# Weight parts placed at different offsets in their buffers, and three orders of wide and narrow products in the up projection

## The chip, the core and the metric

The kernel runs on one core of a Trainium2 chip. The metric is device time in microseconds, the median of several executions. A profile of one execution comes from the hardware profiler; its span runs from the first instruction to the last, and the granted clock of TensorE is shown beside it.

## What is computed

One decoder layer with conditioning, on 256 tokens of width 2048, float32 in and out. A vector c gives shifts, scales and gates; the hidden state goes through an input projection, a retention branch and an HGRN2 branch with gates, an output projection, and then a feed-forward part with a causal convolution of three taps.

```python
mod = silu(c) @ w_ada + b_ada            # shift1, scale1, gate1, shift2, scale2, gate2
h   = rms_norm(x, g_norm1) * (1 + scale1) + shift1
p   = h @ w_in                           # q,k,v,g of retention | q,f,i,g of HGRN2 | gates A, B
yA  = (head_layer_norm(retention(rope(q), rope(k), v)) * silu(g)) @ w_ret_o
yB  = (head_rms_norm(hgrn2(silu(q), f, i)) * silu(g)) @ w_hg_o
x   = x + gate1 * ((sigmoid(gA) * yA + sigmoid(gB) * yB) @ w_out)
h2  = rms_norm(x, g_norm2) * (1 + scale2) + shift2
a, b = split(causal_depthwise_conv3(h2 @ w_up))
x   = x + gate2 * ((silu(a) * b) @ w_down)
out = rms_norm(x, g_final)
```

## The kernel before

**Two parts for each operand.** All large products are made in TensorE's float32r format, from operands split into an upper and a lower part. A weight piece (two tiles of 128 contraction rows by 512 columns) is loaded by SyncE into one of 12 buffers `raw` (`load`, L156 to L159). ScalarE writes the upper part `wh` (L169), VectorE the lower part `wl = raw - wh` (L174). There are 4 buffers each of `wh` and `wl`, 4096 bytes a partition, taken in turn. Activations (`hT`, `og`, `mT`, `h2T`, `gs`) are blocks of 4096 bytes in a pool of 27 (tag `k4`), each holding two contraction tiles, and for each the 256 upper values and then the 256 lower ones. Three products are summed for each tile: upper by upper, lower activation by upper weight, upper activation by lower weight.

**Three forms.** `mm_rows` (L192 to L203) holds the activation as the stationary operand and streams 512 columns of weights: L198 upper activation by wh, L199 lower activation by wh, L203 upper activation by wl. It makes the row groups of the input projection, the branch gates (wab), the branch output projections (whg, wret), the output projection (wout) and the down projection (wdown). `mm_cols` (L205 to L218) holds weights and streams 256 columns of activation, three times. `mm_wide` (L220 to L228) and `up_group` hold weights and stream the 512 columns of an activation tile, both parts at once, against wh (a wide product: L225, L1125), and then 256 columns, the upper part, against wl (a narrow one: L228, L1127).

**The up projection.** `up_group` runs 22 times, once for every two tiles of each half of the 2 x 5632 columns: 16 contraction tiles, 4 output tiles of 128 columns, in PSUM tiles `pg` and `po` by turns. For each contraction tile it makes two wide products, the two narrow ones for the same outputs, and so for the other two outputs. `wide_group` makes the retention's q and k (4 groups) in runs of eight wide and eight narrow products.

**Order.** The matmuls, loads and splits stand in program order per engine, or in an order that the tile scheduler chose from a program traced piece by piece; background work (the conditioning products, which use `raw` buffers too, L458, and the two branches) is pumped in between at a set pace. `pieces` yields a piece's parts after asking for its split.

Of the kernel before, what the change touches and what calls it, by code (L numbers as in the profile page):

```python
# [36 lines left out]
NOSYNC = mybir.DependencyInfo(mybir.DependencyClass.NoSync, mybir.DependencyReason.DATA)  # L37
SMALL = 70

C_RQ, C_RK, C_RV, C_RG, C_HQ, C_HF, C_HI, C_HG = (i * W1 for i in range(8))  # L40
# [17 lines left out]
class Kernel:  # L58
# [96 lines left out]
    def load(self, src, m, w):  # L155
        self.n += 1  # L156
        raw = self.wp.tile([P, m, w], F32, name=f"raw_{self.n}", tag="raw", bufs=12)
        self.pin(self.nc.sync.dma_start(out=raw, in_=src))
# [18 lines left out]

    def pieces(self, src, kts, gain=None):

        uppers = []  # L180
        for k in range(0, kts, 2):
            m = min(2, kts - k)

            while len(uppers) <= k // 2 + (gain is not None) and 2 * len(uppers) < kts:
                at = 2 * len(uppers)
                z = min(2, kts - at)
                uppers.append(self.upper(src[:, at : at + z, :], z, G, gain))
# [41 lines left out]

    def wide_group(self, src, act):  # L230
# [5 lines left out]
        pieces = self.pieces(src, KT)  # L236
# [12 lines left out]

    def products(self, mm, ps, src, act, k0, kts, hold=0, first=True, last=True, gain=None):  # L250

        held = []
        for step in self.pieces(src[:, k0 : k0 + kts, :], kts, gain):
# [11 lines left out]
    def rows(self, src, act, k0=0, kts=KT, ps=None):  # L265
        return self.parts(self.products(self.mm_rows, ps or self.pg(), src, act, k0, kts), True)

# [526 lines left out]
    def run(self):  # L794
# [74 lines left out]
        self.pace(0, 3.5, 24)  # L869

        work = 2 * FIRST
        g = FIRST
# [6 lines left out]
        while min(done) < KT:  # L879
# [7 lines left out]
            if m > 0:  # L887
                self.finish(*ada[:have])
                if g < RESIDENT:
                    self.products(mms[g], ps[g], a["wa"][g], act, done[g], m, first=False, last=have == KT)  # L890
                    if have == KT:
                        take(g, ps[g], True)
                else:
                    take(g, self.products(mms[g], self.pg(), a["wa"][g], act, done[g], m), done[g] == 0)
                done[g] = have
# [45 lines left out]
        for j in range(4):  # L941
            for at, z in self.rows(a["whg"][j], lambda k: og[0][k // 2][:, k % 2, :], 0, 8):
                nc.vector.tensor_tensor(sgb[j][:, at, :], sgb[j][:, at, :], z, ALU.mult)
# [13 lines left out]
        for j in range(4):  # L957
            for at, z in self.rows(a["wret"][j], lambda k: og[1][k // 2][:, k % 2, :], 0, 8):
                nc.vector.tensor_tensor(sga[j][:, at, :], sga[j][:, at, :], z, ALU.mult)
# [15 lines left out]
        for j in range(4):  # L975
# [6 lines left out]
            elif last:  # L982
                g = g3
            ps = self.products(self.mm_rows, self.po2() if last else self.pg(), a["wout"][j], actm, 0, KT, hold=4 * last, gain=g if last else None)
            if last:
                g = None
                self.finish(ada2)
                up = self.pieces(a["wup"][0], KT)
                up = chain([next(up), next(up)], up)
# [68 lines left out]
        for i in range(FT // 2):  # L1058
# [51 lines left out]
    def up_group(self, i, act2, gT, pieces, begun=None):  # L1110
# [6 lines left out]
        else:  # L1117
            ps = [self.po() for _ in range(4)]
        for step in pieces:
            for kt, wh, wl in step:  # L1120
                act = act2(kt)
                for j in range(0, 4, 2):
                    cs = [slice(z * P, (z + 1) * P) for z in (j, j + 1)]
                    for z in range(2):
                        self.pin(nc.tensor.matmul(ps[j + z], lhsT=wh[:, cs[z]], rhs=act, start=kt == 0, stop=False, skip_group_check=bool(begun)))  # L1125
                    for z in range(2):
                        nc.tensor.matmul(ps[j + z][:, :T], lhsT=wl[:, cs[z]], rhs=act[:, :T], start=False, stop=kt == KT - 1, skip_group_check=bool(begun))  # L1127
            self.pump(len(step) / 2)
# [19 lines left out]
    def down(self, gT, x1, g2):  # L1148
# [15 lines left out]
        for j in range(4):  # L1164
# [127 lines left out]
```

## Time and profile before

| what | value |
|---|---|
| median of 3 runs | 1511.69 us (1511.67 to 1511.91) |
| the profiled execution | 1511.24 us |
| its span | 1509.5 us |
| TensorE matmuls | 8466, busy 1493.7 us |
| VectorE | busy 1211.9 us |
| ScalarE | busy 841.7 us |
| mean DMA rate | 256 GB/s |

A row of the page's groups gives the line, the engine, the operation, what is written and read, the count, the busy time, the mean length of one, and the idle time of the engine ahead of it with what ended it. PE is TensorE's matmul, PEld its weight load, which overlaps the matmul. Matmuls overlap each other too, since their recorded length holds their way through the array: the distance from one start to the next is what a stream of them costs, and the sum of lengths is not. The timeline view lists starts and merges equal instructions that follow each other.

### The profile page before, as it was taken

Reading aid. Unit: us, or ns where it says so; the run is one execution under the profiler, and the core shown is the slowest. Engines: PE = TensorE matmul, PEld = TensorE weight load, DVE = VectorE, ACT = ScalarE, POOL = GpSimd, SP = SyncE. Lnnn points to the kernel's source line nnn. Section 1 sums busy time; section 2 is a strip of 40 time slices with the busy share of each in tenths; the row PEclk is TensorE's granted clock in tenths of the full one; section 3 lists DMA queues with packets and bytes.
Section 4 is the critical chain, followed back from the end, with each engine's and each line's share of the span. In section 5 each row is a group of like instructions: output and inputs, shape, how many; then the busy total and the mean of one; then the engine's idle time right before and its main releaser. Section 6 shows DMA issues by size and latency. Waiting matters only on the chain.

```text
span 1509.5 us, 22703 instructions
## 1 busy us (share of the span) xinstructions
PE 1493.7 (99%) x8466; PEld 1275.5 (84%) x8466; DVE 1211.9 (80%) x1647; ACT 841.7 (56%) x1210; POOL 4.0 (0%) x8
## 2 busy tenths in 40 slices
PE   8999999999999999999999999999999999999997
PEld 6889899888888888888888888888888888888886
DVE  7899997998999877898977778777777769455784
ACT  6745456767775644455466555555555658344342
POOL 0000000000000000000000000000000000000000
PEclk9999999999999999999999999999999999999999
DMA  9999997777887899989847777777777666667651
GB/s 373 376 347 336 321 320 257 265 248 274 281 278 262 285 302 326 318 290 361 298 132 242 229 233 230 230 231 238 229 239 231 216 193 204 197 206 212 183 171 56
DMA packets 110994, 385.71 MB, mean 256 GB/s; under 512 B 12802, under 2 KB 13346, under 8 KB 110884
## 3 DMA queue, kind: packets, MB, share of 16 engines
q1 hardware_dynamic: 110016, 383.14, 76.7%
q8 instruction: 66, 1.08, 0.3%
q10 hardware_dynamic: 868, 1.13, 0.2%
q14 instruction: 44, 0.36, 0.1%
HBM read 382.11 MB, written 2.11 MB: 255 GB/s over the span
## 4 chain that ended last, share of the span: by engine, by line
PE 93%; DVE 3%; ACT 1%; issue 1%; DMA 1%; SPq 0%; DVEq 0%; ACTq 0%
PE pg L198 13%; PE pg L203 13%; PE pg L199 13%; PE po L1125 11%; PE pg L1125 10%; PE po L1127 5%; PE pg L1127 5%; PE pg L225 4%; PE po L198 3%; PE po L203 3%; PE po L199 3%; PE pg L228 2%; DVE wl L174 1%; DVE raw L458 1%; PE po L218 1%
## 5 line engine op out<-in xcount | busy, mean ns | idle before, releaser
L174 DVE TENSOR_TENSOR wl<-raw,wh 128x1024 fp32r<-128x1024 f32 (+1 forms) x536 | 633.1, 1191 | 233.6 <-ACT wh L169 230.6
L169 ACT ACTIVATE wh<-raw 128x1024 fp32r<-128x1024 f32 (+1 forms) x536 | 547.9, 1033 | 482.5 <-PE pg L199 167.0
L458 DVE SCALAR_TENSOR_TENSOR raw<-raw,sc 128x1024 f32<-128x1024 f32 x192 | 233.8, 1222 | 0.1
L1125 PE MATMUL po<-h2T,wh 128*128 128x512 f32 x704 | 221.1, 395 | 0.0
L1125 PE MATMUL pg<-h2T,wh 128*128 128x512 f32 x688 | 216.4, 396 | 0.0
L198 PE MATMUL pg<-wh,hT 128*128 128x512 f32 x512 | 202.1, 395 | 0.9 <-DVE p L830 0.6
L199 PE MATMUL pg<-wh,hT 128*128 128x512 f32 x512 | 199.8, 390 | 0.0
L1127 PEld LDWEIGHTS po<-h2T,wl 128*128 128x128 f32 x704 | 132.3, 188 | 31.3
L1127 PEld LDWEIGHTS pg<-h2T,wl 128*128 128x128 f32 x688 | 129.2, 188 | 31.0 <-DVE wl L174 0.5
L203 PE MATMUL pg<-wl,hT 128*128 128x512 f32 x512 | 138.4, 390 | 0.1
L1127 PE MATMUL po<-h2T,wl 128*128 128x256 f32 x704 | 138.3, 278 | 0.0
L1127 PE MATMUL pg<-h2T,wl 128*128 128x256 f32 x688 | 135.3, 278 | 0.1
L198 PEld LDWEIGHTS pg<-wh,hT 128*128 128x128 f32 x512 | 96.1, 188 | 21.3 <-ACT f L579 1.0
L203 PEld LDWEIGHTS pg<-wl,hT 128*128 128x128 f32 x512 | 96.0, 188 | 20.6 <-DVE wl L174 0.4
L199 PEld LDWEIGHTS pg<-wh,hT 128*128 128x128 f32 x512 | 96.2, 188 | 19.6 <-DVE hT L387 0.3
L1125 PEld LDWEIGHTS po<-h2T,wh 128*128 128x128 f32 x704 | 107.2, 189 | 0.0
L1125 PEld LDWEIGHTS pg<-h2T,wh 128*128 128x128 f32 x688 | 104.7, 189 | 0.0
L199 PE MATMUL pg<-wh,gs 128*128 128x512 f32 x176 | 68.6, 390 | 0.0
L198 PE MATMUL pg<-wh,gs 128*128 128x512 f32 x176 | 68.5, 389 | 0.0
L198 PE MATMUL po<-wh,gs 128*128 128x512 f32 x176 | 68.5, 389 | 0.0
L199 PE MATMUL po<-wh,gs 128*128 128x512 f32 x176 | 68.5, 389 | 0.0
L225 PE MATMUL pg<-hT,wh 128*128 128x512 f32 x256 | 65.1, 396 | 0.2 <-DVE p L247 0.2
(255 smaller groups left out, 2023.3 us busy)
## 6 DMA issues: line engine op xcount, KB each, us to landing
raw<-in_wup SPq DMA_DIRECT2D x176, 512.0 KB, 4.5
raw<-in_wdown SPq DMA_DIRECT2D x88, 512.0 KB, 4.2
raw<-in_wa SPq DMA_DIRECT2D x80, 512.0 KB, 5.7
raw<-in_ada SPq DMA_DIRECT2D x64, 512.5 KB, 5.4
raw<-in_ada SPq DMA_DIRECT2D x64, 512.0 KB, 5.5
raw<-in_wab SPq DMA_DIRECT2D x64, 512.0 KB, 5.0
raw<-in_gate SPq DMA_DIRECT2D x32, 512.5 KB, 4.3
raw<-in_wk SPq DMA_DIRECT2D x32, 512.0 KB, 5.1
```

Source lines behind the costliest of these rows:

```text
L169: self.pin(self.nc.scalar.activation(wh, raw, AF.Copy))
L174: self.last = self.nc.vector.tensor_tensor(wl, raw, wh.bitcast(F32), ALU.subtract)
L198: nc.tensor.matmul(ps[t], lhsT=act[:, hi], rhs=wh, start=first and i == 0, stop=False)
L199: nc.tensor.matmul(ps[t], lhsT=act[:, lo], rhs=wh, start=False, stop=False)
L203: nc.tensor.matmul(ps[t], lhsT=act[:, hi], rhs=wl, start=False, stop=last and i == len(items) - 1)
L218: nc.tensor.matmul(outs[j], lhsT=wl[:, cs[j]], rhs=act[:, :T], start=False, stop=last and i == len(items) - 1, skip_group_check=True)
L225: nc.tensor.matmul(ps[z], lhsT=wh[:, z * P : (z + 1) * P], rhs=act, start=first and i == 0, stop=False)
L228: nc.tensor.matmul(ps[z][:, :T], lhsT=wl[:, z * P : (z + 1) * P], rhs=act[:, :T], start=False, stop=last and i == len(items) - 1)
L458: dot = self.pin(nc.vector.scalar_tensor_tensor(raw[:, 0, :], raw[:, 0, :], 1.0, self.sc[:, u * GW : u * GW + w], ALU.mult, ALU.mult, accu ...
L1125: self.pin(nc.tensor.matmul(ps[j + z], lhsT=wh[:, cs[z]], rhs=act, start=kt == 0, stop=False, skip_group_check=bool(begun)))
L1127: nc.tensor.matmul(ps[j + z][:, :T], lhsT=wl[:, cs[z]], rhs=act[:, :T], start=False, stop=kt == KT - 1, skip_group_check=bool(begun))
```

## The change

`wh` and `wl` buffers grow from 4096 to 4352 bytes a partition (64 floats more), and each part starts at a byte offset in its buffer that is set by tables, one pair (for wh, for wl) for each weight group: `COLS` for the four column groups of the input projection, `WIDES` for the four retention groups, `ROWSAT` (the same offset for both parts) for the 20 groups of wab, whg, wret and wout, `UPS` for the 22 groups of the up projection, and `DOWNS` for the four of the down projection. The eight row groups of the input projection stay at offset 0. To make room, `raw` has 11 buffers in place of 12. In `up_group` the first number of a group's entry in `UPS` sets how many wide products run ahead of their narrow ones: 2 as before (groups 0 to 6), 8 (7 to 13), 16 (14 to 18; two pieces are then taken together), or 1 (19 to 21).

```diff
@@ -36,6 +36,16 @@
+ROWSAT = (4, 12, 20, 24, 40, 56, 72, 100, 116, 132, 140, 148, 152, 156, 176, 240, 108, 112, 116, 0)
+UPS = (
+    (2, 192, 192), (2, 64, 192), (2, 192, 64), (2, 144, 64), (2, 0, 64), (2, 48, 64), (2, 64, 160),
+    (8, 0, 64), (8, 0, 0), (8, 0, 192), (8, 144, 64), (8, 192, 64), (8, 192, 192), (8, 64, 64),
+    (16, 0, 64), (16, 144, 64), (16, 192, 64), (16, 0, 160), (16, 0, 192),
+    (1, 0, 0), (1, 64, 64), (1, 192, 192),
+)
+WIDES = ((0, 64), (192, 64), (0, 192), (144, 64))
+COLS = ((64, 64), (160, 160), (192, 192), (8, 8))
+DOWNS = ((0, 64), (64, 0), (0, 112), (0, 0))
...
-        raw = self.wp.tile([P, m, w], F32, name=f"raw_{self.n}", tag="raw", bufs=12)
+        raw = self.wp.tile([P, m, w], F32, name=f"raw_{self.n}", tag="raw", bufs=11)
         self.pin(self.nc.sync.dma_start(out=raw, in_=src))
         return raw
 
-    def upper(self, src, m, w, gain=None):
+    def part(self, name, m, w, shift):
+
+        full = self.wp.tile([P, 2 * G + 64], F32R, name=f"{name}_{self.n}", tag=name, bufs=4)
+        return full[:, shift // 4 : shift // 4 + m * w].rearrange("p (m w) -> p m w", m=m)
+
+    def upper(self, src, m, w, gain=None, shift=(0, 0)):
 
         raw = self.load(src, m, w)
         if gain is not None:
             self.pin(self.nc.vector.tensor_tensor(raw, raw, gain[:, None, :].to_broadcast([P, m, w]), ALU.mult))
         self.n += 1
-        wh = self.wp.tile([P, m, w], F32R, name=f"wh_{self.n}", tag="wh", bufs=4)
-        wl = self.wp.tile([P, m, w], F32R, name=f"wl_{self.n}", tag="wl", bufs=4)
+        wh, wl = [self.part(n, m, w, at) for n, at in zip(("wh", "wl"), shift)]
...
-            begin(self.retention, hb, *[self.wide_group(a["wk"][2 * hb + i], act) for i in range(2)], v.pop(0))
+            begin(self.retention, hb, *[self.wide_group(a["wk"][2 * hb + i], act, WIDES[2 * hb + i]) for i in range(2)], v.pop(0))
...
-            for at, z in self.rows(a["wab"][j], act):
+            for at, z in self.rows(a["wab"][j], act, shift=(ROWSAT[j],) * 2):
...
-            self.up_group(i, act2, gT, up if i == 0 else self.pieces(a["wup"][i], KT), pu if i == 0 else None)
+            self.up_group(i, act2, gT, up if i == 0 else self.pieces(a["wup"][i], KT, shift=UPS[i][1:]), pu if i == 0 else None)
...
+        run = UPS[i][0]
         for step in pieces:
-            for kt, wh, wl in step:
-                act = act2(kt)
-                for j in range(0, 4, 2):
-                    cs = [slice(z * P, (z + 1) * P) for z in (j, j + 1)]
-                    for z in range(2):
-                        self.pin(nc.tensor.matmul(ps[j + z], lhsT=wh[:, cs[z]], rhs=act, start=kt == 0, stop=False, skip_group_check=bool(begun)))
-                    for z in range(2):
-                        nc.tensor.matmul(ps[j + z][:, :T], lhsT=wl[:, cs[z]], rhs=act[:, :T], start=False, stop=kt == KT - 1, skip_group_check=bool(begun))
+            step = list(step)
+            if run == 16 and not begun:
+                step += next(pieces)
+            some = [(kt, act2(kt), wh, wl, z) for kt, wh, wl in step for z in range(4)]
+            for at in range(0, len(some), run):
+                part = some[at : at + run]
+                for kt, act, wh, wl, z in part:
+                    self.pin(nc.tensor.matmul(ps[z], lhsT=wh[:, z * P : (z + 1) * P], rhs=act, start=kt == 0, stop=False, skip_group_check=bool(begun)))
+                for kt, act, wh, wl, z in part:
+                    nc.tensor.matmul(ps[z][:, :T], lhsT=wl[:, z * P : (z + 1) * P], rhs=act[:, :T], start=False, stop=kt == KT - 1, skip_group_check=bool(begun))
...
-            ps = self.products(self.mm_rows, (self.pg, self.po2)[j % 2](), a["wdown"][j], act, 0, FT, hold=8 * last, gain=g if last else None)
+            ps = self.products(self.mm_rows, (self.pg, self.po2)[j % 2](), a["wdown"][j], act, 0, FT, hold=8 * last, gain=g if last else None, shift=DOWNS[j])
```

The calls for `COLS`, for whg, wret and wout, and the parameter that hands an offset pair down (`shift`) through `pieces`, `products`, `rows` and `wide_group`, are changed in the same way.

The order of matmuls on TensorE is the same up to the up projection. At the start of its group 8 (entry 8 in `UPS`; `pg` are the PSUM outputs, `h2T` the activation tile, `wh` and `wl` the weight parts; "x2" stands for two equal rows) TensorE had, before the change:

```order
L1125 MATMUL pg_9236<-h2T_7344,wh_9240 128x512 x2
L1127 MATMUL pg_9236<-h2T_7344,wl_9241 128x256 x2
L1125 MATMUL pg_9237<-h2T_7344,wh_9240 128x512 x2
L1127 MATMUL pg_9237<-h2T_7344,wl_9241 128x256 x2
L1125 MATMUL pg_9236<-h2T_7344,wh_9240 128x512 x2
L1127 MATMUL pg_9236<-h2T_7344,wl_9241 128x256 x2
L1125 MATMUL pg_9237<-h2T_7344,wh_9240 128x512 x2
L1127 MATMUL pg_9237<-h2T_7344,wl_9241 128x256 x2
```

and has now, with line numbers moved by the added lines:

```order
L1147 MATMUL pg_9236<-h2T_7344,wh_9240 128x512 x2
L1147 MATMUL pg_9237<-h2T_7344,wh_9240 128x512 x2
L1147 MATMUL pg_9236<-h2T_7344,wh_9240 128x512 x2
L1147 MATMUL pg_9237<-h2T_7344,wh_9240 128x512 x2
L1149 MATMUL pg_9236<-h2T_7344,wl_9241 128x256 x2
L1149 MATMUL pg_9237<-h2T_7344,wl_9241 128x256 x2
L1149 MATMUL pg_9236<-h2T_7344,wl_9241 128x256 x2
L1149 MATMUL pg_9237<-h2T_7344,wl_9241 128x256 x2
```

The narrow products, which stood behind each two wide ones, now stand behind eight, those of both contraction tiles of a piece.

At the start of group 14, TensorE had two pieces one after the other, of which these are the first and the beginning of the next contraction tiles:

```order
L1125 MATMUL pg_10550<-h2T_7344,wh_10554 128x512 x2
L1127 MATMUL pg_10550<-h2T_7344,wl_10555 128x256 x2
L1125 MATMUL pg_10551<-h2T_7344,wh_10554 128x512 x2
L1127 MATMUL pg_10551<-h2T_7344,wl_10555 128x256 x2
L1125 MATMUL pg_10550<-h2T_7344,wh_10554 128x512 x2
L1127 MATMUL pg_10550<-h2T_7344,wl_10555 128x256 x2
L1125 MATMUL pg_10551<-h2T_7344,wh_10554 128x512 x2
L1127 MATMUL pg_10551<-h2T_7344,wl_10555 128x256 x2
L1125 MATMUL pg_10550<-h2T_7345,wh_10576 128x512 x2
L1127 MATMUL pg_10550<-h2T_7345,wl_10577 128x256 x2
```

and has now the wide products of two pieces (two `wh` buffers) ahead of the first narrow one:

```order
L1147 MATMUL pg_10550<-h2T_7344,wh_10554 128x512 x2
L1147 MATMUL pg_10551<-h2T_7344,wh_10554 128x512 x2
L1147 MATMUL pg_10550<-h2T_7344,wh_10554 128x512 x2
L1147 MATMUL pg_10551<-h2T_7344,wh_10554 128x512 x2
L1147 MATMUL pg_10550<-h2T_7345,wh_10560 128x512 x2
L1147 MATMUL pg_10551<-h2T_7345,wh_10560 128x512 x2
L1147 MATMUL pg_10550<-h2T_7345,wh_10560 128x512 x2
L1147 MATMUL pg_10551<-h2T_7345,wh_10560 128x512 x2
L1149 MATMUL pg_10550<-h2T_7344,wl_10555 128x256 x2
L1149 MATMUL pg_10551<-h2T_7344,wl_10555 128x256 x2
L1149 MATMUL pg_10550<-h2T_7344,wl_10555 128x256 x2
L1149 MATMUL pg_10551<-h2T_7344,wl_10555 128x256 x2
```

The first narrow product moved from the third place to the seventeenth.

In group 19, where the outputs are four tiles `po`, TensorE had:

```order
L1125 MATMUL po_11641<-h2T_7344,wh_11647 128x512
L1125 MATMUL po_11642<-h2T_7344,wh_11647 128x512
L1127 MATMUL po_11641<-h2T_7344,wl_11648 128x256
L1127 MATMUL po_11642<-h2T_7344,wl_11648 128x256
L1125 MATMUL po_11643<-h2T_7344,wh_11647 128x512
L1125 MATMUL po_11644<-h2T_7344,wh_11647 128x512
L1127 MATMUL po_11643<-h2T_7344,wl_11648 128x256
L1127 MATMUL po_11644<-h2T_7344,wl_11648 128x256
```

and has now:

```order
L1147 MATMUL po_11641<-h2T_7344,wh_11647 128x512
L1149 MATMUL po_11641<-h2T_7344,wl_11648 128x256
L1147 MATMUL po_11642<-h2T_7344,wh_11647 128x512
L1149 MATMUL po_11642<-h2T_7344,wl_11648 128x256
L1147 MATMUL po_11643<-h2T_7344,wh_11647 128x512
L1149 MATMUL po_11643<-h2T_7344,wl_11648 128x256
L1147 MATMUL po_11644<-h2T_7344,wh_11647 128x512
L1149 MATMUL po_11644<-h2T_7344,wl_11648 128x256
```

Each narrow product now follows the wide one of the same output, so that consecutive matmuls write the same PSUM tile. On VectorE some splits (`wl`) exchange places with neighbouring steps of the convolution in the up projection; no instruction is added or removed on any engine.

More of the change, by code (lines that the diff above doesn't have):

```diff
@@ L176, in rest, with pieces @@
         return wh, wl
-    def pieces(self, src, kts, gain=None):
+    def pieces(self, src, kts, gain=None, shift=(0, 0)):
         uppers = []
@@ L186, in pieces @@
                 z = min(2, kts - at)
-                uppers.append(self.upper(src[:, at : at + z, :], z, G, gain))
+                uppers.append(self.upper(src[:, at : at + z, :], z, G, gain, shift))
             wh, wl = self.rest(uppers[k // 2])
@@ L228, in mm_wide, with wide_group @@
                 nc.tensor.matmul(ps[z][:, :T], lhsT=wl[:, z * P : (z + 1) * P], rhs=act[:, :T], start=False, stop=last and i == len(items) - 1)
-    def wide_group(self, src, act):
+    def wide_group(self, src, act, shift=(0, 0)):
         nc = self.nc
@@ L235, in wide_group @@
         steps = list(range(0, KT, 4))
-        pieces = self.pieces(src, KT)
+        pieces = self.pieces(src, KT, shift=shift)
         for k in steps:
@@ L248, in wide_group, with products @@
         return out
-    def products(self, mm, ps, src, act, k0, kts, hold=0, first=True, last=True, gain=None):
+    def products(self, mm, ps, src, act, k0, kts, hold=0, first=True, last=True, gain=None, shift=(0, 0)):
         held = []
-        for step in self.pieces(src[:, k0 : k0 + kts, :], kts, gain):
+        for step in self.pieces(src[:, k0 : k0 + kts, :], kts, gain, shift):
             items = [(act(k0 + kt), wh, wl) for kt, wh, wl in step]
@@ L263, in products, with rows @@
         return ps
-    def rows(self, src, act, k0=0, kts=KT, ps=None):
-        return self.parts(self.products(self.mm_rows, ps or self.pg(), src, act, k0, kts), True)
+    def rows(self, src, act, k0=0, kts=KT, ps=None, shift=(0, 0)):
+        return self.parts(self.products(self.mm_rows, ps or self.pg(), src, act, k0, kts, shift=shift), True)
     def put_split(self, dst, src):
@@ L869, in run, with visit @@
         self.pace(0, 3.5, 24)
+        cols = [g for g in range(len(ATT)) if ATT[g] not in ROWS]
+        def visit(g):
+            return COLS[cols.index(g)] if g in cols else (0, 0)
         work = 2 * FIRST
@@ L889, in run @@
                 if g < RESIDENT:
-                    self.products(mms[g], ps[g], a["wa"][g], act, done[g], m, first=False, last=have == KT)
+                    self.products(mms[g], ps[g], a["wa"][g], act, done[g], m, first=False, last=have == KT, shift=visit(g))
                     if have == KT:
@@ L893, in run @@
                 else:
-                    take(g, self.products(mms[g], self.pg(), a["wa"][g], act, done[g], m), done[g] == 0)
+                    take(g, self.products(mms[g], self.pg(), a["wa"][g], act, done[g], m, shift=visit(g)), done[g] == 0)
                 done[g] = have
@@ L941, in run @@
         for j in range(4):
-            for at, z in self.rows(a["whg"][j], lambda k: og[0][k // 2][:, k % 2, :], 0, 8):
+            for at, z in self.rows(a["whg"][j], lambda k: og[0][k // 2][:, k % 2, :], 0, 8, shift=(ROWSAT[8 + j],) * 2):
                 nc.vector.tensor_tensor(sgb[j][:, at, :], sgb[j][:, at, :], z, ALU.mult)
@@ L957, in run @@
         for j in range(4):
-            for at, z in self.rows(a["wret"][j], lambda k: og[1][k // 2][:, k % 2, :], 0, 8):
+            for at, z in self.rows(a["wret"][j], lambda k: og[1][k // 2][:, k % 2, :], 0, 8, shift=(ROWSAT[12 + j],) * 2):
                 nc.vector.tensor_tensor(sga[j][:, at, :], sga[j][:, at, :], z, ALU.mult)
@@ L983, in run @@
                 g = g3
-            ps = self.products(self.mm_rows, self.po2() if last else self.pg(), a["wout"][j], actm, 0, KT, hold=4 * last, gain=g if last else None)
+            ps = self.products(self.mm_rows, self.po2() if last else self.pg(), a["wout"][j], actm, 0, KT, hold=4 * last, gain=g if last else None, shift=(ROWSAT[16 + j],) * 2)
             if last:
@@ L987, in run @@
                 self.finish(ada2)
-                up = self.pieces(a["wup"][0], KT)
+                up = self.pieces(a["wup"][0], KT, shift=UPS[0][1:])
                 up = chain([next(up), next(up)], up)
```

## The prediction, made before the changed kernel ran

> **What bounds the kernel now.** I read the page first: engine totals, slices, chain.
>
> ```profile
> span 1509.5 us, 22703 instructions
> PE 1493.7 (99%) x8466; PEld 1275.5 (84%) x8466; DVE 1211.9 (80%) x1647; ACT 841.7 (56%) x1210; POOL 4.0 (0%) x8
> PEclk9999999999999999999999999999999999999999
> PE 93%; DVE 3%; ACT 1%; issue 1%; DMA 1%; SPq 0%; DVEq 0%; ACTq 0%
> ```
>
> TensorE is busy 99% of the span at a full granted clock, and 93% of the chain that ended last is matmuls. Only some 16 us of the span (1509.5 - 1493.7) have no matmul in them. So the time is a count of matmuls times the distance from one start to the next, and nothing but that distance can be worth much. I read it from the timeline of TensorE, whose first column is the start and whose second is the length in us, in the rows form of the products (a down group, 512 moving columns each) and in the columns form (256 columns).
>
> ```profile
> 1299.43 1.07 PE L203 MATMUL pg<-wl,gs 128*128 128x512 f32 x4
> ...
> 1302.15 1.07 PE L203 MATMUL pg<-wl,gs 128*128 128x512 f32 x4
> ...
> 1304.87 1.07 PE L203 MATMUL pg<-wl,gs 128*128 128x512 f32 x4
> ```
> ```profile
> 30.41 0.64 PE L218 MATMUL pg<-hT,wl 128*128 128x256 f32 x4
> 30.89 0.28 PE L214 MATMUL pg<-hT,wh 128*128 128x256 f32 x1
> ```
>
> From one group of four L203 to the next are 4 + 8 = 12 matmuls in 2.72 us: 226.7 ns each. Four matmuls of 256 columns start 0.48 us apart: 120.0 ns each. The 256 further columns cost 106.7 ns, 0.417 ns per column; what is left is a **constant of 13.3 ns** per matmul (226.7 - 512 x 0.417; 120.0 - 256 x 0.417). That constant is all that a change of addresses can reach. What runs in it is seen by setting the weight loads of TensorE beside the matmuls.
>
> ```profile
> 1300.34 0.39 PE L198 MATMUL pg<-wh,gs 128*128 128x512 f32 x1
> 1300.34 0.19 PEld L199 LDWEIGHTS pg<-wh,gs 128*128 128x128 f32 x1
> ```
>
> The load for the next matmul starts in the same hundredth of a microsecond as the matmul before it, so two reads of the state buffer, moving and stationary, begin together. In the kernel before, both begin at the same residue: wh, wl and every activation tile are blocks of 4096 bytes laid end to end, and slices inside them are multiples of 512 bytes. Whether the constant depends on that distance no row of this trace shows, since in the weight products it is a multiple of 512 bytes. What it shows is that the stall is not the same for like matmuls (lengths in ns, least/median/most):
>
> ```profile
> L1125 PE MATMUL po<-h2T,wh x704: 393/396/398, 794.0 to 1261.7; 128*128 128x512 f32 x176
> L1127 PE MATMUL po<-h2T,wl x704: 274/277/283, 794.4 to 1262.0; 128*128 128x256 f32 x176
> L203 PE MATMUL po<-wl,gs x176: 388/389/389, 1323.9 to 1501.4; 128*128 128x512 f32 x176
> L228 PE MATMUL pg<-hT,wl x256: 277/283/289, 291.3 to 388.6; 128*128 128x256 f32 x128
> ```
>
> 512 columns take from 388 to 398 ns, 256 columns from 274 to 283 in one stage: a **spread of 9 to 10 ns** that hangs on what is loaded beside them and when. In the rows form all are alike (389), although their distances run through several multiples of 512.
>
> **The change, part by part.**
>
> *Offsets.* They change no count and no shape. I counted pairs (matmul, and the load of the next one that runs beside it) in the changed kernel's order: of 7424 pairs of weight products, 4999 get a distance that is no multiple of 256 bytes; 2425 keep one that is. What a pair gains or loses has no row. Bounds from the nearest: the spread of 9 ns, either way, for every shifted pair: -9 x 4999 = -45.0 us to +45.0 us. The nearest row is the steady 389 ns, unmoved by distances of 512, 1024 and 2048 bytes, so I stay near zero, and below it, since both reads now begin at the same residue, the start at which two streams collide if place matters at all, while the narrow products show that 9 ns less can be had. I take a fifth of the spread: -1.8 x 4999 = **-9.0 us**.
>
> The Trainium skill (TensorE: Matmul & The Clock Gate, section Back-to-back issue gap) gives a warm matmul its columns divided by 2.4 GHz plus about 2.5 ns. The trace agrees on the columns (0.417 ns) and has 13.3 in place of 2.5; if the shifted pairs all fell to the page's figure, an estimate by it is 10.8 x 4999 = 54 us less.
>
> *Order in the up projection.* Seven groups keep pairs (2 wide, 2 narrow), seven go to eight and eight, five to sixteen, three to one and one. Pairs and eights both stand in the trace: the up projection, and the retention projections (L225, L228).
>
> ```profile
> 1000.17 0.63 PE L1125 MATMUL pg<-h2T,wh 128*128 128x512 f32 x2
> ...
> 1011.32 0.62 PE L1125 MATMUL pg<-h2T,wh 128*128 128x512 f32 x2
> ```
> ```profile
> 302.49 1.11 PE L228 MATMUL pg<-hT,wl 128*128 128x256 f32 x8
> ...
> 308.08 1.11 PE L228 MATMUL pg<-hT,wl 128*128 128x256 f32 x8
> ```
>
> Pairs: 11.15 us over 16 cycles, 696.9 ns for two wide and two narrow. Eights: 5.59 us for two cycles, 698.8 ns for the same work. A group has 32 such cycles, so eights cost 7 x 32 x 1.9 ns = **+0.4 us**. Sixteens tend to the steady 2 x 226.7 + 2 x 120.0 = 693.3 ns: between -0.6 and +0.3 us for five groups, taken as 0. One and one has no row; a pair of wide and narrow may land anywhere in the spread, 3 x 64 x 9 ns = 1.7 us either way, taken as 0 because pairs and eights differ so little.
>
> *One buffer of raw weights fewer, larger parts.* SyncE waits for a free raw tile almost all the time, and that is its slack:
>
> ```profile
> SPq L158 <- DVE wl L174: 866.5, 491, 7.1
> raw<-in_wa SPq DMA_DIRECT2D x80, 512.0 KB, 5.7
> 30.00:120.00 90.00, 89.71 (x466) 76.75 (x466) 79.90 (x105) 53.77 (x79) 0.95 (x1) 1.00 0.98 364
> 290.00:390.00 100.00, 99.75 (x917) 87.41 (x916) 94.14 (x132) 66.79 (x106) 1.91 (x2) 1.00 0.82 277
> 790.00:1230.00 440.00, 440.00 (x2528) 383.89 (x2527) 335.35 (x504) 248.76 (x376) 0.00 (x0) 1.00 0.73 230
> ```
>
> (Windows: length, busy us of PE, weight loads, DVE, ACT, POOL, clock, DMA share, GB/s.) Where transfers are densest, 30 to 120 us, 364 GB/s move one 524,288-byte tile in 1.44 us; eleven tiles are 15.8 us ahead of a landing that takes 5.7. The later loads have longer. Where loads and splits exchange places with neighbours, the same cover holds. Price 0; the cover is those 10 us, and if it is gone each late tile costs TensorE up to 1.4 us.
>
> *ACT and DVE on shifted parts.* They write and read wh and wl at the new starts. No row has such a start. The split on DVE takes 1224 ns in the median and at most 1271:
>
> ```profile
> L174 DVE TENSOR_TENSOR wl<-raw,wh x536: 670/1224/1271, 17.4 to 1491.1; 128x1024 fp32r<-128x1024 f32 x167, 128x512 fp32r<-128x512 f32 x12
> ```
>
> At +47 ns a piece, 176 pieces of the up projection add 8.3 us to a DVE that is busy 335 of 440 us there: hidden by matmuls. The thin cover is 290 to 390 us (DVE 94.1 of 100): 32 pieces, at most 1.5 us. A gain there has the same bound, and TensorE, not DVE, sets the end. Price 0.
>
> Sum: 1511.24 (the profiled execution, 1509.5 span and 1.7 around it) - 9.0 + 0.4 = 1502.6 us. The median of the runs shown is 1511.69, 0.03% above that execution; I leave it there.
>
> **The rivals.**
>
> *No effect (same).* The constant is the price of any load beside a matmul, whatever its place. For it: the rows form stands at 389 ns through all distances it has. Against: the spread in the up projection, though that may come from timing alone. Price: order alone, -1.9 to +2.4 us about 1511.6. The Trainium skill speaks for it (SBUF — State Buffer, section SBUF: two separate sides): TensorE has ports of its own and never waits on anyone, and its two read ports are independent. By that rule the offsets give 1511.6; the trace's 13.3 ns does not decide it.
>
> *Slower: shifted reads settle at the long end.* Like matmuls already show 398 ns in place of 389 in the up projection. If a distance that is no multiple of 256 makes that the steady state in a fifth of the shifted pairs more than are relieved, the price is 9 x 1000 = +9.0 us: 1520.6. It decides from the point where more pairs lengthen than shorten; then rows-form groups show matmuls over 389 ns. For it: of the wide products in the up projection all but few are on the long side, so 389 may be the lucky state; against it: nothing shows that place makes it.
>
> *The change hardly does what it says.* 2425 pairs, among them all eight row groups of the first projection, keep multiples of 256; if those alone decided, the result is that of no effect.
>
> **How the numbers follow.** Faster as forecast 0.42 (1502.6; its own range from 1476, -9 ns x four fifths of the shifted pairs, up to 1508), no effect 0.31 (1511.6), slower 0.27 (1520.6, its tail to the +45 bound). About 0.2% (3 us) is what a measurement of this kernel can tell from no change; so faster 0.42, same 0.31, slower 0.27. The range that leaves out two in ten, mostly the far ends of -45 and +45: 1482 to 1523 us.
>
> **What would show it.** In the changed profile the groups have one offset each, so the timeline tells each apart. Right: row groups with offsets start every 217 to 226 ns in place of 226.7, and differ from each other, while the unshifted down group (the last) stays at 226.7. No effect: 226.7 everywhere. Slower: lengths over 389 in the rows form. Order: a group of eights with both offsets 0 takes 32 x 0.699 = 22.4 us, one of ones with both 0 within 0.6 us of that. Buffers: PE idle on a transfer between 30 and 120 us would show that term wrong. The forecast fails if the offset's effect has one sign for nearly all distances, since then a fifth of the spread is far too little, or the wrong side.

## The result, and the profile after

The changed kernel takes 1523.35 us in the median of 3 runs (1522.72 to 1523.99), against 1511.69 us: a ratio of 1.0077, 95% interval 1.0054 to 1.0100. It is slower by 0.8%; the forecast was 1502.6 us and faster.

First the page of the changed kernel: span, engine totals, granted clock by slices, and the chain that ended last.

```profile
span 1521.5 us, 22677 instructions
...
PE 1504.9 (99%) x8466; PEld 1277.9 (84%) x8466; DVE 1209.5 (79%) x1647; ACT 841.3 (55%) x1210; POOL 4.0 (0%) x8
...
PEclk9999999999999999999999999999999999999999
...
PE 93%; DVE 2%; DMA 2%; ACT 2%; issue 1%; SPq 0%; DVEq 0%; ACTq 0%
```

The picture is that of before: TensorE busy for 99% of the span, the same 8466 matmuls, the same clock, 93% of the chain. Its busy time is 11.2 us longer (1504.9 - 1493.7) in a span that is 12.0 us longer. So no engine has become a new bound; the same matmuls follow each other at a greater distance. The view of what TensorE waited for agrees (longest waits of the changed kernel; total, times, longest):

```profile
PE po L228 <- ACT hT L396: 2.4, 2, 1.2
PE po L310 <- DMA crow<-in_c: 2.3, 1, 2.3
PE po L363 <- DVE rq L359: 1.9, 1, 1.9
```

All its waits sum to 8.6 us in eight entries, and to 7.7 us in eight before, seven of them the same. The loss must be in the stream. The view by line gives the lengths of like matmuls (least/median/most, ns) and the first and last start. One row of the kernel before, and three of the changed one (L203 is now L217):

```profile
L203 PE MATMUL pg<-wl,og x128: 387/389/398, 588.9 to 676.8; 128*128 128x512 f32 x128
```
```profile
L217 PE MATMUL pg<-wl,gs x176: 387/394/397, 1273.8 to 1453.6; 128*128 128x512 f32 x176
...
L217 PE MATMUL po<-wl,gs x176: 388/389/397, 1334.9 to 1513.5; 128*128 128x512 f32 x176
...
L217 PE MATMUL pg<-wl,og x128: 390/396/404, 593.2 to 683.7; 128*128 128x512 f32 x128
```

The two branch projections (`og`) ran from 588.9 to 676.8, 87.9 us; they now take 90.5 us (593.2 to 683.7), and not one of their 128 products with wl is as short as the old median of 389 ns: the least is 390. In the down projection the median of `pg`, groups 0 and 2, whose wl start at 64 and 112, is 394, while `po`, groups 1 and 3, whose wl both start at 0, keeps 389. The timeline shows it in single groups (start, length). First wab's last group, offset 100, then the down projection's last, offset 0:

```profile
575.98 1.12 PE L217 MATMUL pg<-wl,hT 128*128 128x512 f32 x4
...
578.86 1.12 PE L217 MATMUL pg<-wl,hT 128*128 128x512 f32 x4
```
```profile
1480.15 1.07 PE L217 MATMUL po<-wl,gs 128*128 128x512 f32 x4
...
1482.87 1.07 PE L217 MATMUL po<-wl,gs 128*128 128x512 f32 x4
```

Twelve matmuls in 2.88 us against twelve in 2.72: **240.0 ns each at offset 100, 226.7 at offset 0**. The constant of 13.3 ns has doubled to 26.6.

Summed over the whole trace, by weight groups (distance from each matmul's start to the next one's, added up in ns and given in us; the group of a matmul follows from its place in the program's order):

| products | before | after | difference |
|---|---|---|---|
| rows: wab | 178.06 | 183.55 | +5.49 |
| rows: whg and wret | 87.82 | 90.49 | +2.66 |
| rows: wout | 87.40 | 89.26 | +1.87 |
| rows: down | 239.24 | 241.56 | +2.32 |
| columns of the input projection | 96.49 | 95.09 | -1.40 |
| retention's q and k | 91.36 | 91.19 | -0.17 |
| up projection | 491.66 | 492.62 | +0.96 |

The rows form alone has +12.3 us, as much as the whole span has grown. What holds weights as the stationary operand is nearly even.

Two rows of the up projection in the changed kernel, wide and narrow:

```profile
L1147 PE MATMUL po<-h2T,wh x704: 387/392/403, 802.6 to 1271.5; 128*128 128x512 f32 x176
```
```profile
L1149 PE MATMUL po<-h2T,wl x704: 276/281/286, 803.0 to 1271.8; 128*128 128x256 f32 x176
```

The wide ones are 4 ns shorter in the median (396 before), the narrow ones 4 ns longer (277 before): gains and losses that cancel over 22 groups. The split on VectorE, which writes and reads the shifted parts, did not change (1224 and 1271 ns before):

```profile
L188 DVE TENSOR_TENSOR wl<-raw,wh x536: 666/1221/1278, 17.6 to 1503.2; 128x1024 fp32r<-128x1024 f32 x167, 128x512 fp32r<-128x512 f32 x12
```

### The profile page after: what moved, and what is told of

Read it like the earlier page. It is cut to its first block, busy times and chain, and to the rows that moved or that the text cites. A ratio compares the mean times of both kernels' runs of the same rounds, so it can differ in the third digit from the quotient of the medians.

```text
span 1521.5 us, 22677 instructions
## 1 busy us (share of the span) xinstructions
PE 1504.9 (99%) x8466; PEld 1277.9 (84%) x8466; DVE 1209.5 (79%) x1647; ACT 841.3 (55%) x1210; POOL 4.0 (0%) x8
## 4 chain that ended last, share of the span: by engine, by line
PE 93%; DVE 2%; DMA 2%; ACT 2%; issue 1%; SPq 0%; DVEq 0%; ACTq 0%
PE pg L212 13%; PE pg L217 13%; PE pg L213 13%; PE po L1147 11%; PE pg L1147 10%; PE po L1149 5%; PE pg L1149 5%; PE pg L239 4%; PE po L212 3%; PE po L213 3%; PE po L217 3%; PE pg L242 2%; PE pg L229 1%; PE pg L228 1%; PE pg L232 1%; DVE wl L188 1%
## 5 line engine op out<-in xcount | busy, mean ns | idle before, releaser
L213 PE MATMUL pg<-wh,hT 128*128 128x512 f32 x512 | 201.7, 394 | 0.0
L1147 PE MATMUL po<-h2T,wh 128*128 128x512 f32 x704 | 199.7, 393 | 0.0
L1147 PE MATMUL pg<-h2T,wh 128*128 128x512 f32 x688 | 193.0, 395 | 0.0
L217 PE MATMUL pg<-wl,hT 128*128 128x512 f32 x512 | 140.6, 394 | 0.1
L1147 PEld LDWEIGHTS po<-h2T,wh 128*128 128x128 f32 x704 | 122.8, 188 | 18.7
L1147 PEld LDWEIGHTS pg<-h2T,wh 128*128 128x128 f32 x688 | 118.5, 188 | 16.3
L1149 PE MATMUL po<-h2T,wl 128*128 128x256 f32 x704 | 125.9, 280 | 0.0
L1149 PEld LDWEIGHTS po<-h2T,wl 128*128 128x128 f32 x704 | 110.9, 188 | 11.3
L1149 PEld LDWEIGHTS pg<-h2T,wl 128*128 128x128 f32 x688 | 107.2, 188 | 14.4 <-DVE wl L188 0.6
L1149 PE MATMUL pg<-h2T,wl 128*128 128x256 f32 x688 | 116.9, 281 | 0.1
L217 PEld LDWEIGHTS pg<-wl,hT 128*128 128x128 f32 x512 | 96.6, 189 | 21.8 <-DVE wl L188 0.4
L213 PEld LDWEIGHTS pg<-wh,hT 128*128 128x128 f32 x512 | 96.7, 189 | 20.9 <-DVE hT L401 0.3
L213 PE MATMUL pg<-wh,gs 128*128 128x512 f32 x176 | 68.8, 391 | 0.0
L213 PE MATMUL po<-wh,gs 128*128 128x512 f32 x176 | 68.8, 391 | 0.0
```

The costliest lines, as they stand in the source:

```text
L213: nc.tensor.matmul(ps[t], lhsT=act[:, lo], rhs=wh, start=False, stop=False)
L217: nc.tensor.matmul(ps[t], lhsT=act[:, hi], rhs=wl, start=False, stop=last and i == len(items) - 1)
L1147: self.pin(nc.tensor.matmul(ps[z], lhsT=wh[:, z * P : (z + 1) * P], rhs=act, start=kt == 0, stop=False, skip_group_check=bool(begun)))
L1149: nc.tensor.matmul(ps[z][:, :T], lhsT=wl[:, z * P : (z + 1) * P], rhs=act[:, :T], start=False, stop=kt == KT - 1, skip_group_check=bool(be ...
```

## The experiments

The questions were, one after the other: do the offsets of the rows form make the whole loss (theory A), or do the larger buffers or the up projection make some of it? And, in the rows form, is it the **distance** between the start of the moving operand and the start of the next stationary one that decides (theory D), or **where the moving operand starts** (theory M)? In the changed kernel both change together, since weights at offset s move past activations at offset 0: the distance is then no multiple of 256, and the start itself is shifted. "Distance" is always meant modulo 256 bytes below. The means are those of a group's distances from start to start, with pauses over 300 ns left out.

### 1. Only the rows form back at offset 0

```diff
-ROWSAT = (4, 12, 20, 24, 40, 56, 72, 100, 116, 132, 140, 148, 152, 156, 176, 240, 108, 112, 116, 0)
+ROWSAT = (0,) * 20
-DOWNS = ((0, 64), (64, 0), (0, 112), (0, 0))
+DOWNS = ((0, 0),) * 4
```

> The changed kernel with every offset of the rows form at 0 (branch gates, branch outputs, output and down projection); offsets of the columns form, the retention groups and the up projection, its orders and the eleven raw buffers stay. Theory A (the loss lies in the rows form, where the shifted weights are the moving operand): the starts of these groups in the two profiles differ by 12.4 us in sum, so 1523.35 - 12.4 = 1510.9 us, and all rows groups start every 226.7 ns again. Theory B (the loss comes from the larger buffers, one raw buffer fewer or the orders in the up projection, and the rows only show it): at most half comes back, 1517 us or more.

Measured: 1510.63 us, against 1511.36 for the kernel before on the same chip; ratio 0.9995 (0.9985 to 1.0004). The whole loss is gone, with every other offset and order still there. The row by line of this kernel:

```profile
L217 PE MATMUL pg<-wl,gs x176: 389/389/389, 1263.0 to 1440.4; 128*128 128x512 f32 x176
```

All alike at 389 ns, as before the change. The columns have -1.7 us and the up projection +1.0 us here, so they nearly cancel.

### 2. Only the buffers

```diff
-COLS = ((64, 64), (160, 160), (192, 192), (8, 8))
+COLS = ((0, 0),) * 4
```

and so for the other four tables, with all 22 groups of the up projection in pairs: what is left of the change is larger parts and 11 raw buffers.

> All offsets 0 and pairs in every up group; what is left of the change is the 4352-byte parts and the eleven raw buffers. Theory A: 1511.7 us, within 1 us of the kernel before, since distances are multiples of 256 bytes and loads have slack. Theory B (buffers cost something): 1514 us or more, with TensorE idle on a transfer or on a split between 30 and 300 us.

Measured: 1511.37 against 1511.36 us, ratio 1.0003 (0.9993 to 1.0013). The window where transfers are densest, in this kernel (length, busy us of PE, weight loads, DVE, ACT, POOL, clock, DMA share, GB/s):

```profile
30.00:120.00 90.00, 89.71 (x466) 76.69 (x465) 79.80 (x106) 53.64 (x78) 0.95 (x1) 1.00 0.99 358
```

TensorE is busy for 89.71 of 90 us, the same as before: the missing raw buffer is not felt.

### 3. A scan of offsets

```diff
+ROWSAT = (16, 32, 48, 64, 80, 96, 128, 144, 160, 192, 208, 224, 8, 28, 44, 60, 240, 176, 36, 84)
+COLS = ((4, 4), (12, 12), (24, 24), (40, 40))
+DOWNS = ((4, 4), (8, 8), (64, 64), (128, 128))
```

The tables of the retention and up groups were changed too, to offsets of 0, 4, 8, 12, 24, 40, 72 and 136 bytes.

> Other offsets in every group, to complete the table: rows form at multiples of 16, and at 8, 28, 36, 44, 60, 84 bytes; columns form at 4, 12, 24 and 40; retention and up groups at 0, 4, 8, 12, 24, 40, 72 and 136 in pairs, eights and sixteens. If the place within 16 bytes decides (theories D and M alike), rows at 36, 84 and 4 stand at 240 ns, at 28, 44, 60 at 229 to 231, at 8 at 233 to 235, and all multiples of 16 at one value between 226.7 and 231. If the place within 256 bytes decides, multiples of 16 differ among themselves by more than 5 ns and 4, 36 and 84 do not agree. Columns form: 24 and 40 (8 modulo 16) stand at 115 to 116 ns as 8 did, 4 and 12 on either side of 120. Total about 1520 us.

One run, 1529.03 us, 9 us more than was expected. No rows group with an offset came near 226.7 ns: multiples of 16 gave 229 to 235 (64: 229.4, 16: 231.6, 128: 232.4, 208: 234.5), starts 12 past a multiple of 16 gave 229 to 230, those 8 past gave 233, those 4 past 235 to 238. So a start on a multiple of 16 isn't enough: its distance still costs. Nor does the offset alone set the price: 64 cost 229.4 ns in wab and 233.3 in the down projection. A full group of the up projection took 22.12 to 22.56 us (22.29 at 0). For the columns a guess of mine was missed: 24 and 40 gave 121.9 and 119.1 ns (120 at 0), so the gain seen at offset 8 in the changed kernel (115.6) is not one of all starts 8 past a multiple of 16.

### 4. The two theories apart, a first try

```diff
-                z = self.blk([P, 2, 2 * T], F32R, name="gs")
+                z = self.blk([P, 4 * T + 16], F32R, name="gs")[:, GSAT // 4 : GSAT // 4 + 4 * T].rearrange("p (j t) -> p j t", j=2)
```

with `GSAT = 12`, and `DOWNS = ((12, 12), (0, 0), (16, 16), (8, 8))`: the activation of the down projection is moved too, so that distance and start can be chosen apart.

> As the kernel with all offsets 0, but the activation tiles of the down projection (gs, the stationary operand there) start 12 bytes into their blocks, and the weight parts of its four groups at 12, 0, 16 and 8 bytes. Matmul starts in steady runs, group by group. Theory D (the distance from the moving to the stationary operand decides, modulo 16): distances 0, 12, 12 and 4, so 226.7, 240, 240 and 229 to 231 ns. Theory M (the start of the moving operand alone decides, modulo 16): 229 to 231, 226.7, 226.7 to 231 and 233 to 235 ns. Theory S (the start of the stationary operand alone): all four alike and away from 226.7 ns.

One run, 1524.65 us: 231.3, 232.4, 233.3 and 234.0 ns for the four groups. This is neither theory's pattern. The fault was in the kernel: the activation blocks had become 4160 bytes, 65 times 64, so distances ran through all multiples of 64 from tile to tile, whatever the offsets. The run decides nothing between D and M. It shows one thing all the same: in wab, whg, wret and wout, whose weights start at 0, the groups rose to means of 230 to 232 ns (226.7 to 228.6 before), so a start on a multiple of 16, even of 64, isn't enough by itself. The next two have blocks of 4352 bytes, a multiple of 256, and 9 raw buffers to make room.

### 5. Activation at 4

The edit of experiment 4 with `4 * T + 64`, `GSAT = 4`, and `DOWNS = ((4, 4), (0, 0), (8, 8), (20, 20))`.

> All offsets 0 but in the down projection. Activation blocks are 4352 bytes here (and raw has nine buffers), so that distances between blocks stay multiples of 256 bytes. The stationary gs starts 4 bytes into its block in all four groups; the weights (moving) start at 4, 0, 8 and 20 bytes. Distances moving to stationary: 0, 4, -4, -16. Theory D (what matters is that the distance is a multiple of 256): the first group 226.7 ns, all others above 229. Theory M (the moving operand's own start within 16 bytes): 240, 226.7, 233 and 240 ns.

One run, 1520.17 us. The timeline of its down groups 0, 2 and 3 (L213 is the product with wl):

```profile
1289.28 1.11 PE L213 MATMUL pg<-wl,gs 128*128 128x512 f32 x4
...
1292.13 1.11 PE L213 MATMUL pg<-wl,gs 128*128 128x512 f32 x4
```
```profile
1409.96 1.09 PE L213 MATMUL pg<-wl,gs 128*128 128x512 f32 x4
...
1412.75 1.09 PE L213 MATMUL pg<-wl,gs 128*128 128x512 f32 x4
```
```profile
1472.13 1.12 PE L213 MATMUL po<-wl,gs 128*128 128x512 f32 x4
...
1475.01 1.12 PE L213 MATMUL po<-wl,gs 128*128 128x512 f32 x4
```

Twelve matmuls take 2.85, 2.79 and 2.88 us: 237.5, 232.5 and 240.0 ns; the means of whole groups are 237.2, 232.8 and 239.9, and 232.4 for group 1. Group 0 has distance 0 and is slow: D alone falls. Group 1 has weights at 0, as in the kernel before, but the distance is 4: it is slow too, and M alone falls. Both matter. The unshifted wout groups, whose activations also lie in blocks of 4352 bytes, stay at 226.7 (three of the four; the first has 227.9, and 227.6 before the change), so odd multiples of 256 are as good as even ones.

### 6. Activation at 64

The same kernel with `GSAT = 64` and `DOWNS = ((64, 64), (0, 0), (128, 128), (68, 68))`.

> As the run before, with gs 64 bytes into its block and the weights at 64, 0, 128 and 68 bytes. Theory D: 226.7 ns in the first group, 229 to 235 in the second and third, where the distance is 64 bytes either way; the fourth (distance 4, moving operand 4 past a line) above 229. Theory M: 226.7 in the first three (all start on multiples of 16), 240 in the fourth.

One run, 1516.47 us. Down groups 0, 1 and 3 in the timeline:

```profile
1291.24 1.07 PE L213 MATMUL pg<-wl,gs 128*128 128x512 f32 x4
...
1293.96 1.07 PE L213 MATMUL pg<-wl,gs 128*128 128x512 f32 x4
```
```profile
1349.13 1.09 PE L213 MATMUL po<-wl,gs 128*128 128x512 f32 x4
...
1351.93 1.09 PE L213 MATMUL po<-wl,gs 128*128 128x512 f32 x4
```
```profile
1471.68 1.11 PE L213 MATMUL po<-wl,gs 128*128 128x512 f32 x4
...
1474.53 1.11 PE L213 MATMUL po<-wl,gs 128*128 128x512 f32 x4
```

2.72, 2.80 and 2.85 us: 226.7, 233.3 and 237.5 ns (means 226.7, 233.3, 237.6; group 2, with distance 64 the other way and a start at 128, has 228.9). This is the clearest pair of the study. With both operands shifted by 64 nothing is lost; with weights back at 0, where they had been fast, 6.6 ns are. So in the rows form the steady 226.7 ns were seen only where the distance is a multiple of 256 *and* the moving operand starts on a multiple of 16; a start 4 past it costs some 10 ns even where the distance is 4 or 0.

### 7. Order and offsets in the up projection, and more rows

```diff
+ROWSAT = (52, 68, 164, 180, 196, 212, 228, 244, 76, 92, 124, 172, 188, 204, 220, 236, 252, 120, 136, 200)
+UPS = ((1, 0, 0), (4, 0, 0), (2, 0, 0), (8, 0, 0), (16, 0, 0),
+    (1, 192, 192), (2, 192, 192), (4, 192, 192), (8, 192, 192), (16, 192, 192), ...
```

> A table again, for the order at equal offsets and for more places. Order theory (runs of one cost, longer runs save): at offsets 0 a group of 128 matmuls takes 22.6 us in ones, 22.3 in pairs and eights, 22.2 in sixteens; at 192 the same order on a level 0.2 us lower from eights on. If the order does nothing, all are within 0.1 us at equal offsets. Rows form: 52, 68, 164, 180, 196, 212, 228, 244 (4 modulo 16) at 233 to 240 ns; 76, 92, 124, 172, 188, 204, 220, 236, 252 (12 modulo 16) at 229 to 231; 120, 136, 200 at 233. Columns form: 8, 72, 200, 56 (all 8 modulo 16) at 115 to 116 ns if the place within 16 bytes sets it.

One run, 1525.04 us. The timeline of a rows group 4 past a multiple of 16 (offset 68) and one 12 past (76):

```profile
415.41 1.12 PE L212 MATMUL pg<-wl,hT 128*128 128x512 f32 x4
...
418.29 1.12 PE L212 MATMUL pg<-wl,hT 128*128 128x512 f32 x4
```
```profile
594.59 1.08 PE L212 MATMUL pg<-wl,og 128*128 128x512 f32 x4
...
597.34 1.08 PE L212 MATMUL pg<-wl,og 128*128 128x512 f32 x4
```

240.0 and 229.2 ns (2.88 and 2.75 us for twelve). All eight groups 4 past had means of 235 to 239, all nine 12 past 229 to 231. The down groups, whose offsets were (0, 0), (16, 16), (128, 0) and (0, 128) here, had 226.9, 231.7, 232.2 and 229.4. In the up projection a group of 128 matmuls took, by order, at offsets (0, 0): pairs 22.31, fours 22.44, eights 22.35, sixteens 22.27 us; at (192, 192): ones 22.60, pairs 22.11, fours 22.15, eights 22.11, sixteens 22.14. From pairs on, the order is worth 0.2 us a group at most; ones cost 0.5 us at 192, and 0.3 us at 0 in the changed kernel (22.62 against 22.29). For the columns, 56, 72 and 200 gave 117.7 to 119.0, and 8 again 115.8: a rule for these isn't found. Their means are not sharper than some 1 ns: offset 192 gave 117.7 in the changed kernel and 116.5 in experiment 1, which left it where it was.

### 8. The moving start where activations move

Does the cost of a start 4 past a multiple of 16 belong to weights, or to any moving operand? Here the activation of the up projection is moved by 4 (`H2AT`, blocks of 4352 bytes, 9 raw buffers), rows and columns are at 0.

```diff
-                h2T.append(self.blk([P, 2, 2 * T], F32R, name="h2T"))
+                h2T.append(self.blk([P, 4 * T + 64], F32R, name="h2T")[:, H2AT // 4 : H2AT // 4 + 4 * T].rearrange("p (j t) -> p j t", j=2))
```

> All weight offsets 0 outside the up projection, activation blocks of 4352 bytes, nine raw buffers. The up projection's activation h2T, its moving operand, starts 4 bytes into its block; the weights there at 4, 0, 196 or 12 bytes in pairs, eights and sixteens. Theory M in its general form (a moving operand 4 bytes past a multiple of 16 is slow, whatever it holds): wide products start every 236 to 240 ns and narrow ones every 120 to 127, so a group of 128 matmuls takes 22.8 us or more at every weight offset, also where the distance is 0, and the run is 12 us or more slower. Rival (it is something about the weight parts: how they are written or read at such a place): groups with weights at 4 take 22.3 us as with everything at 0, and groups at 196 take 22.05 us as they did at 192.

One run, 1526.82 us against 1511.1 on its chip. In group 7, of eights with weights at (4, 4), so distance 0:

```profile
938.34 1.14 PE L1145 MATMUL po<-h2T,wl 128*128 128x256 f32 x8
...
941.21 1.14 PE L1145 MATMUL po<-h2T,wl 128*128 128x256 f32 x8
```

2.87 us for eight wide and eight narrow products, where eights at 0 took 5.59 / 2 = 2.80 us before the change. All full groups, whatever their weights' offset, took 22.78 to 23.15 us in place of 22.29. That it is the moving operand's start, and not the stationary one's at 4 too, experiment 3 shows: with the same weights at (4, 4) and the activation at 0, a group took 22.20 us in pairs, 22.40 in eights and 22.43 in sixteens, against 23.15, 23.00 and 23.00 here. The cost belongs to the moving operand.

### 9. A kernel of the good places

```diff
+ROWSAT = (0,) * 20
+UPS = ((8, 192, 192),) * 22
+WIDES = ((192, 192),) * 4
+COLS = ((8, 8),) * 4
+DOWNS = ((0, 0),) * 4
```

> Offsets only where weights are stationary: columns form 8 and 8, retention and up groups 192 and 192 in runs of eight; rows form at 0. From the group sums of the two profiles: up 2784 x -1.9 ns = -5.3 us, columns form 768 x -4.4 ns = -3.4 us, retention -0.8 us: 1511.4 - 9.5 = 1502 us, ratio 0.9937, if what single groups gained adds up. If the gain of a group hung on its neighbours or on chance, 1508 to 1512 us.

Measured in 5 runs: **1502.48 us** (1502.17 to 1503.55) against 1510.95, ratio 0.9943 (0.9929 to 0.9957). It beats both kernels. The page's head, and a piece of the up projection in its timeline:

```profile
span 1501.7 us, 22668 instructions
...
PE 1485.1 (99%) x8466; PEld 1271.1 (85%) x8466; DVE 1208.6 (80%) x1647; ACT 837.9 (56%) x1210; POOL 4.0 (0%) x8
```
```profile
999.75 1.07 PE L1144 MATMUL pg<-h2T,wl 128*128 128x256 f32 x8
...
1002.49 1.11 PE L1144 MATMUL pg<-h2T,wl 128*128 128x256 f32 x8
...
1005.27 1.07 PE L1144 MATMUL pg<-h2T,wl 128*128 128x256 f32 x8
```

Two cycles in 5.52 us, 2.76 each, where eights at 0 took 2.80. Summed over the trace, the up projection has -5.6 us, the columns -2.7, retention -0.6, the rows form +0.2 and all the rest +1.1: together -7.6, against a span shorter by 7.8 us.

## Why the prediction was wrong

**The bound** was right: TensorE's distance from start to start was all that the change could reach, and all the time came from there.

**The step that failed is the offset term**: "I take a fifth of the spread: -1.8 x 4999 = -9.0 us". Its *sign* was chosen because "both reads now begin at the same residue, the start at which two streams collide if place matters at all". Experiment 6 shows the opposite for the rows form: where the moving operand starts on a multiple of 16, the same residue is the best place found, and 64 bytes of difference cost 6.6 ns. Its *bound* of 9 ns a pair, the spread of lengths before the change, was too tight: at offset 100 a pair lost 13.3.

And it took all 4999 shifted pairs as *one population*. They are at least two. The 1440 matmuls of the shifted wab, whg, wret and wout groups lost 10.0 us (5.49 + 2.66 + 1.87), 7.0 ns each; down lost 2.3 us; the columns gained 1.4 us, and retention and up moved by 1 us and less. The rows of the table add up to +11.7 us; some 1.2 of them are the order's (an estimate from the group times of experiment 7 and the changed kernel: 0.05 us in each of seven eights, 1.0 in the three ones, nearly nothing in the sixteens), so the term was about +10.5 us in place of -9.0. One price for all could only be right by luck; the term worth forming was a price for each form, times its own count.

The steady 389 ns under distances of 512, 1024 and 2048 bytes was read as a sign that place matters little. It was a sample of multiples of 256 only, and experiment 6 shows what that hid: the row that seemed neutral was the one good state of its form.

**The rival that held** is "shifted reads settle at the long end", 1520.6 us. Its own mark was lengths over 389 ns in the rows form, and there they are (396 in the median of `og`). Its price, +9.0 us, was 2.7 us too small, and that it came so near is luck: it was worked out as 9 ns on a fifth of all shifted pairs, whereas 1440 in the rows form lost 7.0 ns each and the columns gained. The range ended at 1523, 0.35 us under the time.

**No effect** fell. The Trainium skill (SBUF — State Buffer, section SBUF: two separate sides) speaks for it, with two independent read ports for TensorE; down group 1 speaks against it, with weights at 0 both times: 226.7 ns with the activation at 0 (experiment 2), 233.3 with it at 64 (experiment 6). The measurement decides, though no run shows that the ports are what makes the difference.

The estimate of 54 us, from a gap of 2.5 ns, leaves out a condition: the Trainium skill (TensorE: Matmul & The Clock Gate, section Back-to-back issue gap) gives that figure for an isolated matmul, and says that in a stream of weight loads and matmuls both set the spacing. No steady stream in the changed kernel came near 2.5: the nearest, such as the narrow products of group 13, started every 113 ns, some 6 over the 106.7 of their 256 columns.

**The change hardly does what it says** was right on the first projection's eight row groups (227.1 ns in the mean, 227.0 before) and wrong on the rest.

**Order** was right in the eights and sixteens: eights at offset 0 took 22.34 us (forecast 22.4), sixteens 22.27 to pairs' 22.31. Ones were taken as 0; they cost 0.3 us a group, 1.0 us in three, inside the bound of 1.7.

**Buffers** were right: experiment 2, and no idle of TensorE on a load of weights in the changed kernel. **ACT and DVE on shifted parts** were right too: the split on DVE takes 1221 ns in the median in place of 1224, that on ACT 1061 in place of 1062.

Of the marks that were named beforehand, the unshifted last down group did keep 226.7 ns, and the shifted ones did differ from each other, but upward, 227 to 240 in place of 217 to 226.

Left open: what in the chip makes a distance of 256 the period, why some distances cost 2 ns and others 8, why the down groups (0, 112) and (0, 64) differ (227.2 and 231.2 ns), why one offset costs 4 ns more in one group than in another (64 in experiment 3), and a rule for the columns and the up projection, where (8, 8) and (192, 192) are only the best of the places tried.

## What to carry to other kernels

Where TensorE is the bound and each matmul brings its own weight load, look at the distance between moving operand and next stationary one as at a tunable: place both on multiples of 256 first, and treat another place as a thing to be measured form by form, since the same offset (8) lost 7 ns with weights moving (233.3 against 226.7) and gained 4 with weights held (115.7 against 120.0). A flat row of the profile says nothing of values that it doesn't contain, so before a price is put on a new kind of place, one group of each form is worth a run. And one price for thousands of unlike pairs hides that gains and losses may cancel.

## What was not expected of the hardware

- For 512 moving columns of this format the distance from start to start ran from 226.7 to 240.0 ns by place alone. By the start of the moving operand past a multiple of 16 bytes: 0 with distance 0, 226.7 in groups without pauses, and up to 228.9 where other work breaks in; 0 with another distance, 229 to 235 (both parts shifted alike); 12 past, 229 to 231; 8 past, 232 to 235; 4 past, 233 to 240.
- 256 moving columns went both ways from 120.0: 115.7 at offset 8, 121.9 at 24; in the up projection the steady narrow ones fell to 113 (group 13, offsets 64, 64), while the wide ones there rose to 233 in the mean.
- A change inside a sequence has a price of its own: in the down group (0, 64) the first products with wh after those with wl, though at distance 0, started 231, 236, 228, 233 and 231 ns apart before they came back to 226 and 227. Before the change the same is seen where wide products follow narrow ones: 234, 236, 228, 232, 231, then 227.
